# A masked-reconstruction loss on one core: the last columns taken singly, in parts and on another engine

## The chip, the cores and the metric

The kernel runs on one core of a Trainium2 chip. The time is that of the device for one execution, in microseconds. Nine runs of the kernel before have a median of 79.06 us (78.79 to 80.93). One further execution was recorded by the profiler; it took 79.05 us.

## The reference

Two float32 arrays `pred` and `target` of shape 32 x 147 x 768 come in, and 32 numbers go out, one for each batch entry:

```
mean = target.mean(axis=-1, keepdims=True)
var = target.var(axis=-1, keepdims=True)
target = (target - mean) / np.sqrt(var + 1e-6)
loss = np.mean((pred - target) ** 2, axis=-1)
return loss.mean(axis=-1).astype(np.float32)
```

Each of the 4,704 rows of 768 elements is normalised by its own mean and variance, the squared difference to `pred` is averaged over the row, and the 147 rows of an entry are averaged. Both inputs together are 28.9 MB, read once.

## The kernel before

**Tiling.** The 128 partitions hold 32 entries by 4 row groups. A "column" c is one row of 768 elements on each partition. There are 36 full columns, 0 to 35 (`KM` is 36), and one, `REST` = 36, of 96 partitions. So one column of one input is 393 KB in memory.

**Loads.** The list `stream` (lines 55 to 61) names the pieces in order: "t" for target, "p" for pred, first and last column, and the queue. The target's columns 36 and 0 to 3 come as float32 over SyncE's queue ("hw"). All others come over GpSimd's queue ("sw"), which casts them to bf16 on the way. Most pieces are four columns, the last of each input are two, and the pred columns 34 and 35 are single. There are eight completion semaphores for the sw loads, used in turn, which are called lanes here: a load waits on its lane until the load eight places before it has landed. It does so on GpSimd, where the next work queues behind it.

**The work on one column.** VectorE takes the statistics of the target (`stats`, lines 125 to 145: two `bn_stats` over 384 elements each, one `bn_aggr`). For a group of columns (`groups`: fours, and pairs from column 28 on) ScalarE takes the root of the variance and VectorE its reciprocal r, and the product nmr = -mean * r (line 144). GpSimd writes the normalised target to a bf16 tile s as target * r + nmr (`normalise`, line 158). TensorE forms pred minus s in PSUM with two products, by the negated identity `nident` for s and by the identity `ident` for pred (`subtract`, line 179). ScalarE squares the result in place and sums it along the row (`square`, line 185). A unit (`units`, line 63) is what one PSUM tile z and one square cover: two columns, except for 36, 34 and 35. There are two z tiles in turn. At the end TensorE adds the row sums by entry: products with a 0/1 mask that is scaled by 1/(147 * 768) (`sums`, lines 187 to 195). VectorE copies the 32 numbers out of PSUM (line 229) and SyncE stores them.

**Order.** Every instruction is put on record with a due time by `at`, from hand-set landing times and durations (lines 197 to 223), and all are issued in order of due time (line 225). Each engine runs its own queue strictly in that order, so an instruction that waits holds all behind it.

Of the kernel before, what the change touches and what calls it, by code (L numbers as in the profile page):

```python
# [14 lines left out]
def kernel(  # L15
# [24 lines left out]
    def rows_of(c):  # L40
        return RP if c == REST else P

    def dram(x, c0, c1):
        return bass.AP(tensor=x.tensor, offset=x.offset + c0 * D,
                       ap=[[N * D, B], [KJ * D, J - 1 if c0 == REST else J], [1, (c1 - c0) * D]])

    data = ctx.enter_context(tc.tile_pool(name="data", bufs=1))
    work = ctx.enter_context(tc.tile_pool(name="work", bufs=10))
    small = ctx.enter_context(tc.tile_pool(name="small", bufs=8))
# [2 lines left out]
    psum1 = ctx.enter_context(tc.tile_pool(name="psum1", bufs=1, space=bass.MemoryType.PSUM))  # L52


    stream = [("t", REST, REST + 1, "hw"), ("t", 0, 4, "hw"), ("p", REST, REST + 1, "sw")]
    stream += [("t", 4, 8, "sw"), ("t", 8, 12, "sw"), ("p", 0, 4, "sw")]
    for c in range(12, KM - 4, 4):
        stream += [("t", c, c + 4, "sw"), ("p", c - 8, c - 4, "sw")]
    stream += [("t", KM - 4, KM - 2, "sw"), ("p", KM - 12, KM - 8, "sw"), ("t", KM - 2, KM, "sw"),
               ("p", KM - 8, KM - 6, "sw"), ("p", KM - 6, KM - 4, "sw"), ("p", KM - 4, KM - 2, "sw"),  # L60
               ("p", KM - 2, KM - 1, "sw"), ("p", KM - 1, KM, "sw")]

    units = [(REST,)] + [(c, c + 1) for c in range(0, KM - 2, 2)] + [(KM - 2,), (KM - 1,)]

    groups = [(REST,)] + [tuple(range(c, c + 4)) for c in range(0, KM - 8, 4)]
    groups += [(c, c + 1) for c in range(KM - 8, KM, 2)]


    land, issue = {}, []
    t = 2.7  # L70
    for kind, c0, c1, q in stream:
        t += (c1 - c0) * D * 4 * rows_of(c0) / 430e3
        issue.append(t + 1.0)
        for c in range(c0, c1):
            land[kind, c] = t + 1.0

    todo = []

    def at(when, fn):
        todo.append((when, len(todo), fn))  # L80

    tbuf, pbuf, sbuf, rs = {}, {}, {}, {}

    def load(kind, c0, c1, q):
        x = targ_f if kind == "t" else pred_f
        n = rows_of(c0)
        til = data.tile([P, (c1 - c0) * D], F32 if q == "hw" else BF16, name=f"{kind}{c0}")
        eng = nc.sync if q == "hw" else nc.gpsimd
        pin(eng.dma_start(out=til[:n], in_=dram(x, c0, c1)))  # L89
        for c in range(c0, c1):  # L90
            (tbuf if kind == "t" else pbuf)[c] = (til, (c - c0) * D)

    lanes = [0.0] * 8
    k = 0
    for i, piece in enumerate(stream):
        if piece[3] == "hw":
            at(-1.0, lambda piece=piece: load(*piece))
        else:
            at(lanes[k % 8] + (0.01 * k), lambda piece=piece: load(*piece))
            lanes[k % 8] = issue[i] + 0.2  # L100
            k += 1

    ident = singles.tile([P, P], BF16)
    nident = singles.tile([P, P], BF16)
    mask = singles.tile([P, B], F32)
    mask_rest = singles.tile([P, B], F32)
    eps_t = singles.tile([P, 1], F32)

    def constants():
        pin(nc.vector.memset(eps_t, eps))  # L110
        for til, v in ((ident, 1.0), (nident, -1.0)):
            pin(nc.gpsimd.memset(til, 0.0))  # L112
            pin(nc.gpsimd.affine_select(out=til, in_=til, compare_op=ALU.not_equal, fill=v,  # L113
                                        base=0, pattern=[[-1, P]], channel_multiplier=1))
        for m, per, n in ((mask, J, P), (mask_rest, J - 1, RP)):
            pin(nc.gpsimd.memset(m, 1.0 / (N * D)))
            pin(nc.gpsimd.affine_select(out=m[:n], in_=m[:n], compare_op=ALU.is_ge, fill=0.0,
                                        base=0, pattern=[[-per, B]], channel_multiplier=1))
            pin(nc.gpsimd.affine_select(out=m[:n], in_=m[:n], compare_op=ALU.is_ge, fill=0.0,
                                        base=per - 1, pattern=[[per, B]], channel_multiplier=-1))  # L120

    at(1.0, constants)


    def stats(g):
        n, K = rows_of(g[0]), len(g)
        r = small.tile([P, K], F32, name="r")
        nmr = small.tile([P, K], F32, name="nmr")
        for i, c in enumerate(g):
            rs[c] = (r[:n, i:i + 1], nmr[:n, i:i + 1])  # L130
        if not norm_pix_loss:
            pin(nc.vector.memset(r, 1.0))
            pin(nc.vector.memset(nmr, 0.0))
            return
        mv = small.tile([P, K, 2], F32, name="mv")
        for i, c in enumerate(g):
            til, o = tbuf[c]
            st = small.tile([P, 2, 6], F32, name="st")
            for j in range(2):
                pin(nc.vector.bn_stats(out=st[:n, j, :], in_=til[:n, o + j * half:o + (j + 1) * half]))  # L140
            pin(nc.vector.bn_aggr(out=mv[:n, i], in_=st[:n]))  # L141
        pin(nc.scalar.activation(out=r[:n], in_=mv[:n, :, 1], func=ACTF.Sqrt, bias=eps_t[:n], scale=1.0))  # L142
        pin(nc.vector.reciprocal(out=r[:n], in_=r[:n]))  # L143
        pin(nc.vector.scalar_tensor_tensor(out=nmr[:n], in0=mv[:n, :, 0], scalar=-1.0,  # L144
                                           in1=r[:n], op0=ALU.mult, op1=ALU.mult))


    def normalise(u, i):
        c = u[i]
        n = rows_of(c)  # L150
        if i == 0:
            s = work.tile([P, 2 * D], BF16, name="s")
            for m, cc in enumerate(u):
                sbuf[cc] = (s, m * D)
        s, so = sbuf[c]
        til, o = tbuf[c]
        r, nmr = rs[c]
        pin(nc.gpsimd.tensor_scalar(out=s[:n, so:so + D], in0=til[:n, o:o + D], scalar1=r, scalar2=nmr,  # L158
                                    op0=ALU.mult, op1=ALU.add))


    main_units = [u for u in units if u[0] != REST]
    early = len(main_units) - 4
    rl = singles.tile([P, len(main_units)], F32)
    rl_rest = singles.tile([P, 1], F32)
    rl_sum = singles.tile([P, 1], F32)
    acc = psum1.tile([1, B], F32)
    zs = {}

    def subtract(u):  # L170
        n, W = rows_of(u[0]), len(u) * D
        z = psum.tile([P, 3 * BANK], F32, name="z")
        zs[u] = z
        s = sbuf[u[0]][0]
        ptil, po = pbuf[u[0]]
        for src, so, w, first in ((s, 0, nident, True), (ptil, po, ident, False)):
            for a in range(0, W, BANK):
                b = min(a + BANK, W)
                pin(nc.tensor.matmul(z[:n, a:b], w[:n, :n], src[:n, so + a:so + b], start=first, stop=not first))  # L179

    def square(u):
        n, W = rows_of(u[0]), len(u) * D
        z = zs[u]
        to = rl_rest[:n] if u[0] == REST else rl[:, main_units.index(u):main_units.index(u) + 1]
        pin(nc.scalar.activation(out=z[:n, :W], in_=z[:n, :W], func=ACTF.Square, accum_out=to))  # L185

    def sums(a, b):

        if a == "rest":
            pin(nc.tensor.matmul(acc, rl_rest[:RP], mask_rest[:RP], start=False, stop=False))  # L190
        elif a == 0:
            pin(nc.vector.tensor_reduce(out=rl_sum, in_=rl[:, 0:b], axis=mybir.AxisListType.X, op=ALU.add))  # L192
            pin(nc.tensor.matmul(acc, rl_sum, mask, start=True, stop=False))
        else:
            pin(nc.tensor.matmul(acc, rl[:, a:b], mask, start=False, stop=b == len(main_units)))  # L195

    dve = pool = pe = act = 0.0
    ready = {}
    for g in groups:
        dve = max([dve] + [land["t", c] for c in g])  # L200
        at(dve, lambda g=g: stats(g))
        dve += 1.26 * len(g) + 0.8
        for c in g:
            u = next(u for u in units if c in u)
            pool = max(pool, dve + 0.1)
            at(pool, lambda u=u, i=u.index(c): normalise(u, i))
            pool += 1.1
            ready[c] = pool + 0.1
    free = [0.0, 0.0]
    for u in units:  # L210
        pe = max([pe, free[0]] + [ready[c] for c in u] + [land["p", c] for c in u])
        at(pe, lambda u=u: subtract(u))
        pe += 0.7 * len(u)
        act = max(act, pe + 0.3)
        at(act, lambda u=u: square(u))
        act += 0.65 * len(u) + 0.35
        free = [free[1], act]
        i = main_units.index(u) if u in main_units else -1
        if i == early - 1:
            at(act + 3.0, lambda: sums(0, early))  # L220
            at(act + 3.0, lambda: sums("rest", None))
        elif i >= early:
            at(act + (3.1 if i < len(main_units) - 1 else 5.0), lambda i=i: sums(i, i + 1))

    for when, order, fn in sorted(todo, key=lambda e: e[:2]):
        fn()

    ob = singles.tile([1, B], F32)
    nc.vector.tensor_copy(out=ob, in_=acc)  # L229
    nc.sync.dma_start(out=out, in_=ob[0, :])  # L230


# [33 lines left out]
```

## Time and profile before

| | |
|---|---|
| median of nine runs | 79.06 us |
| the profiled execution | 79.05 us |
| its span, first to last instruction | 77.3 us |
| busy: TensorE, VectorE, ScalarE, GpSimd | 37.9, 45.9, 32.5, 50.3 us |
| read from memory | 28.90 MB |
| last input piece landed | 72.19 us |
| final product begins | 74.90 us |

The page's row "DMA" cuts the span into 40 slices of 1.93 us and shows the busy share of the 16 DMA engines in tenths. Lines of the timeline give start, duration, engine, source line, operation and tiles, and in brackets the idle time of the engine before it and what ended that. PE is TensorE, PEld its weight load, DVE is VectorE, ACT ScalarE, POOL GpSimd and SP SyncE. The landing of each load is read from the trace's semaphore records: a load has landed when the last of its 16 engines has reported.

### The profile page before, as it was taken

The numbers are of one execution on the slowest core, as the hardware profiler recorded it, in microseconds if no ns is written. First come the engines' busy times: TensorE is split into PE (matmuls) and PEld (weight loads), VectorE is DVE, ScalarE is ACT, GpSimd is POOL, SyncE is SP. The second block draws the span as 40 slices with busy tenths as digits, with TensorE's granted clock in tenths as the row PEclk, the third lists the DMA queues.
The fourth block names the chain that finished last, engine by engine and source line by source line (L and its number), as shares of the span: only waits on it lengthen the run. The fifth ranks groups of instructions, "written<-read, shape, count | busy, mean of one in ns | idle before, by whom it ended". The sixth has DMA issues, their size and how long they took to land.

```text
span 77.3 us, 601 instructions
## 1 busy us (share of the span) xinstructions
PE 37.9 (49%) x124; PEld 13.2 (17%) x126; DVE 45.9 (59%) x138; ACT 32.5 (42%) x53; POOL 50.3 (65%) x73
## 2 busy tenths in 40 slices
PE   0000250005990029979052982597079669467740
PEld 0000120001230013323011330232023123022310
DVE  0061009979979799799699339916797718400000
ACT  5001000050010194492790646095307395698960
POOL 4998902029959989899599699359887763180000
PEclk9999999999999655599975559857965999999999
DMA  0899999999999999999999999999999999997000
GB/s 0 184 407 299 312 238 219 210 216 213 219 210 223 207 216 217 216 213 213 216 213 219 210 216 217 216 216 210 203 223 223 197 210 213 218 199 128 2 0 0
DMA packets 3398, 15.43 MB, mean 200 GB/s; under 512 B 386, under 2 KB 738, under 8 KB 3266
## 3 DMA queue, kind: packets, MB, share of 16 engines
q0 software_dynamic: 3136, 13.52, 86.3%
q1 hardware_dynamic: 258, 1.87, 6.4%
q14 instruction: 3, 0.02, 0.1%
q8 instruction: 1, 0.02, 0.1%
HBM read 28.90 MB, written 0.00 MB: 374 GB/s over the span
## 4 chain that ended last, share of the span: by engine, by line
DMA 43%; DVE 32%; ACT 8%; POOL 5%; issue 5%; PE 2%; SPq 1%; another core or an unknown queue 0%; ACTq 0%
DMA p<-in_pred_dram 30%; DVE st L140 24%; DMA t<-in_target_dram 13%; ACT z L185 7%; DVE mv L141 5%; POOL s L158 4%; PE z L179 2%; ACT r L142 2%; DVE r L143 1%; DVE nmr L144 1%; SPq L89 1%; POOL t L89 1%; PE acc L195 0%; DVE ob L229 0%
## 5 line engine op out<-in xcount | busy, mean ns | idle before, releaser
L140 DVE BATCH_NORM_STATS2 st<-t 128x6 f32<-128x384 bf16 (+2 forms) x74 | 36.3, 533 | 14.4 <-DMA t<-in_target_dram 14.4
L158 POOL TENSOR_SCALAR s<-t,r,nmr 128x768 bf16<-128x768 bf16 (+2 forms) x37 | 36.1, 981 | 13.1 <-DVE nmr L144 12.8
L179 PE MATMUL z<-s,nident 128*128 128x512 bf16 (+3 forms) x57 | 21.2, 487 | 27.9 <-POOL s L158 25.0
L185 ACT ACTIVATE z<-z 128x1536 f32<-128x1536 f32 (+2 forms) x20 | 26.7, 1336 | 2.7 <-PE z L179 2.3
L179 PE MATMUL z<-p,ident 128*128 128x512 bf16 (+3 forms) x55 | 19.7, 472 | 8.5 <-DMA p<-in_pred_dram 8.3
L142 ACT ACTIVATE r<-mv,eps_t 128x4 f32<-128x4 f32 (+2 forms) x12 | 3.6, 297 | 38.9 <-DVE mv L141 38.9
L179 PEld LDWEIGHTS <-nident 128*128 128x128 bf16 (+1 forms) x57 | 5.9, 120 | 40.4 <-ACT z L185 16.3
L89 POOL DMA_DIRECT2D p<-in_pred_dram x13 | 7.7, 595 | 5.2 <-DMA t<-in_target_dram 3.2
L179 PEld LDWEIGHTS <-ident 128*128 128x128 bf16 (+1 forms) x57 | 6.8, 120 | 19.9 <-issue 17.1
L141 DVE BATCH_NORM_AGGREGATE mv<-st 128x2 f32<-128x12 f32 (+1 forms) x37 | 7.7, 209 | 1.3
L89 POOL DMA_DIRECT2D t<-in_target_dram x9 | 5.3, 590 | 0.0
L143 DVE RECIPROCAL r<-r 128x4 f32<-128x4 f32 (+2 forms) x12 | 2.1, 172 | 4.6 <-ACT r L142 4.6
L185 ACT ACTIVATION_READ_ACCUMULATOR z<-z 128x1 f32 (+1 forms) x20 | 3.7, 185 | 0.0
L229 DVE COPY ob<-acc 1x32 f32<-1x32 f32 x1 | 0.2, 178 | 5.3 <-PE acc L195 5.3
L144 DVE SCALAR_TENSOR_TENSOR nmr<-mv,r 128x4 f32<-128x4 f32 (+2 forms) x12 | 1.9, 161 | 0.4
L192 DVE TENSOR_REDUCE rl_sum<-rl 128x1 f32<-128x15 f32 x1 | 0.2, 169 | 2.6 <-ACT z L185 2.6
L142 ACT ACT_TABLE_LOAD x1 | 1.3, 1283 | 0.8 <-PEq L247 0.8
L195 PE MATMUL acc<-mask,rl 128*1 128x32 f32 x8 | 0.6, 192 | 0.8 <-ACT z L185 0.8
L110 DVE MEMSET eps_t<- 128x1 f32 x1 | 0.1, 59 | 0.9 <-PEq L247 0.9
L195 PEld LDWEIGHTS acc<-mask,rl 128*1 128x1 f32 x8 | 0.3, 82 | 1.2 <-ACT z L185 0.9
L112 POOL MEMSET ident<- 128x128 bf16 x1 | 0.4, 361 | 0.0
L113 POOL TENSOR_SCALAR_AFFINE_SELECT ident<-ident 128x128 bf16<-128x128 bf16 x1 | 0.3, 294 | 0.1
(16 smaller groups left out, 2.6 us busy)
## 6 DMA issues: line engine op xcount, KB each, us to landing
t<-in_target_dram POOLq DMA_DIRECT2D x7, 768.0 KB, 25.8
p<-in_pred_dram POOLq DMA_DIRECT2D x7, 768.0 KB, 26.4
t<-in_target_dram SPq DMA_DIRECT2D x1, 1536.0 KB, 9.9
p<-in_pred_dram POOLq DMA_DIRECT2D x3, 384.0 KB, 23.1
t<-in_target_dram POOLq DMA_DIRECT2D x2, 384.0 KB, 25.7
p<-in_pred_dram POOLq DMA_DIRECT2D x2, 192.0 KB, 16.5
t<-in_target_dram SPq DMA_DIRECT2D x1, 288.0 KB, 3.7
p<-in_pred_dram POOLq DMA_DIRECT2D x1, 144.0 KB, 3.7
```

The lines of the kernel that those rows point to most:

```text
L89: pin(eng.dma_start(out=til[:n], in_=dram(x, c0, c1)))
L112: pin(nc.gpsimd.memset(til, 0.0))
L113: pin(nc.gpsimd.affine_select(out=til, in_=til, compare_op=ALU.not_equal, fill=v, base=0, pattern=[[-1, P]], channel_multiplier=1))
L140: pin(nc.vector.bn_stats(out=st[:n, j, :], in_=til[:n, o + j * half:o + (j + 1) * half]))
L141: pin(nc.vector.bn_aggr(out=mv[:n, i], in_=st[:n]))
L142: pin(nc.scalar.activation(out=r[:n], in_=mv[:n, :, 1], func=ACTF.Sqrt, bias=eps_t[:n], scale=1.0))
L143: pin(nc.vector.reciprocal(out=r[:n], in_=r[:n]))
L144: pin(nc.vector.scalar_tensor_tensor(out=nmr[:n], in0=mv[:n, :, 0], scalar=-1.0, in1=r[:n], op0=ALU.mult, op1=ALU.mult))
L158: pin(nc.gpsimd.tensor_scalar(out=s[:n, so:so + D], in0=til[:n, o:o + D], scalar1=r, scalar2=nmr, op0=ALU.mult, op1=ALU.add))
L179: pin(nc.tensor.matmul(z[:n, a:b], w[:n, :n], src[:n, so + a:so + b], start=first, stop=not first))
L185: pin(nc.scalar.activation(out=z[:n, :W], in_=z[:n, :W], func=ACTF.Square, accum_out=to))
L195: pin(nc.tensor.matmul(acc, rl[:, a:b], mask, start=False, stop=b == len(main_units)))
```

## The change

- **Pieces of the stream.** The pred columns 20 to 27 are loaded by pairs, 30 to 34 singly. Column 35 is loaded as 512 and then 256 elements of each row, into tiles of their own. The target's columns 32 and 33 are moved ahead of the pred columns 20 to 23, and 34 and 35 to just behind these. Target 0 to 3 is put ahead of target 36.
- **Units.** Columns 30 to 35 are units of their own. Column 35 is two units of 512 and 256 elements, with a square each.
- **Columns 31 and 34 go to VectorE.** It writes pred minus s to a bf16 tile in SBUF, takes its mean and variance by `bn_stats` and `bn_aggr`, and forms mean squared plus variance. The mask for these two sums is `mask_mean`, which is `mask` times 768.
- **Scales.** The product nmr goes. ScalarE writes minus the mean (a Copy with scale -1) behind each root, and GpSimd computes (target - mean) * r. The groups of columns 28 to 35 are pairs, as before; their statistics, root and reciprocal are now separate steps that can be put between others.
- **Order.** The due times are replaced by a list planner: each step has an engine, a duration, the steps that it needs, a rank and an earliest time, and the step that can start first is issued next. The target product of a unit is a step of its own, and may run before the pred has landed.

In the planned order, VectorE's work at the end is the difference and statistics of column 31, the sum over the early units, and the difference and statistics of column 34. TensorE's ends with the two products of column 35's first part, the sums of columns 31 and 32, the two products of its second part, and the sums of 33, of both parts of 35 and of 34. ScalarE's order is: root of (34,35), squares of (26,27) and (28,29), and then of 30, 32, 33 and both parts of 35. GpSimd issues the loads of 30 to 35 one by one between the normalisations of columns 24 to 31.

```diff
-    stream = [("t", REST, REST + 1, "hw"), ("t", 0, 4, "hw"), ("p", REST, REST + 1, "sw")]
-    stream += [("t", 4, 8, "sw"), ("t", 8, 12, "sw"), ("p", 0, 4, "sw")]
+    piece("t", 0, 4, q="hw")
+    piece("t", REST, REST + 1, q="hw")
+    piece("t", 4, 8)
+    piece("p", REST, REST + 1)
+    piece("t", 8, 12)
+    piece("p", 0, 4)
     for c in range(12, KM - 4, 4):
-        stream += [("t", c, c + 4, "sw"), ("p", c - 8, c - 4, "sw")]
-    stream += [("t", KM - 4, KM - 2, "sw"), ("p", KM - 12, KM - 8, "sw"), ("t", KM - 2, KM, "sw"),
-               ("p", KM - 8, KM - 6, "sw"), ("p", KM - 6, KM - 4, "sw"), ("p", KM - 4, KM - 2, "sw"),
-               ("p", KM - 2, KM - 1, "sw"), ("p", KM - 1, KM, "sw")]
+        piece("t", c, c + 4)
+        if c == KM - 8:
+            piece("t", KM - 4, KM - 2)
+        if c < KM - 8:
+            piece("p", c - 8, c - 4)
+        else:
+            piece("p", c - 8, c - 6)
+            piece("p", c - 6, c - 4)
+    piece("t", KM - 2, KM)
+    for c in range(KM - 12, KM - 6, 2):
+        piece("p", c, c + 2)
+    for c in range(KM - 6, KM - 1):
+        piece("p", c, c + 1)
+    piece("p", KM - 1, KM, 0, BANK)
+    piece("p", KM - 1, KM, BANK, D)
...
-    units = [(REST,)] + [(c, c + 1) for c in range(0, KM - 2, 2)] + [(KM - 2,), (KM - 1,)]
+    units = [((c, c + 1), 0, D, "ACT") for c in range(0, KM - 6, 2)]
+    units.insert(2, ((REST,), 0, D, "ACT"))
+    units += [((KM - 6 + i,), 0, D, eng) for i, eng in enumerate(("ACT", "DVE", "ACT", "ACT", "DVE"))]
+    units += [((KM - 1,), 0, BANK, "ACT"), ((KM - 1,), BANK, D, "ACT")]
...
-        pin(nc.vector.scalar_tensor_tensor(out=nmr[:n], in0=mv[:n, :, 0], scalar=-1.0,
-                                           in1=r[:n], op0=ALU.mult, op1=ALU.mult))
+        pin(nc.scalar.activation(out=nm[:n], in_=mv[:n, :, 0], func=ACTF.Copy, scale=-1.0))
...
-        pin(nc.gpsimd.tensor_scalar(out=s[:n, so:so + D], in0=til[:n, o:o + D], scalar1=r, scalar2=nmr,
-                                    op0=ALU.mult, op1=ALU.add))
+        pin(nc.gpsimd.tensor_scalar(out=s[:n, so:so + D], in0=til[:n, o:o + D], scalar1=nm, scalar2=r,
+                                    op0=ALU.add, op1=ALU.mult))
...
+    def difference(u):
+        z = zs[u] = work.tile([P, D], BF16, name="zd")
+        s, so = sbuf[u[0]]
+        til, o = pred_of(u[0], 0)
+        pin(nc.vector.tensor_tensor(out=z, in0=til[:, o:o + D], in1=s[:, so:so + D], op=ALU.subtract))
+
+    def mean_of_squares(u, dest):
+        z = zs[u]
+        mv = small.tile([P, 2], F32, name="mvz")
+        bn(mv, [z[:, 0:half], z[:, half:D]])
+        pin(nc.vector.scalar_tensor_tensor(out=dest, in0=mv[:, 0:1], scalar=mv[:, 0:1], in1=mv[:, 1:2],
+                                           op0=ALU.mult, op1=ALU.add))
...
+    while left:
+        best = None
+        for i in left:
+            name, engine, dur, needs, fn, rank, early = ops[i]
+            if any(x not in end for x in needs):
+                continue
+            t = max([free[engine], early] + [end[x] + (0.0 if ops[by_name[x]][1] == engine else HOP) for x in needs])
+            key = (t, rank, i)
+            if best is None or key < best[0]:
+                best = (key, i)
```

## The prediction

> **What bounds the kernel now.** I read the page's span and DMA queues first, then the chain of waits, then the timeline of the last 15 us, then the busy times in short windows at the end.
>
> ```profile
> span 77.3 us, 601 instructions
> PE 37.9 (49%) x124; PEld 13.2 (17%) x126; DVE 45.9 (59%) x138; ACT 32.5 (42%) x53; POOL 50.3 (65%) x73
> DMA  0899999999999999999999999999999999997000
> ```
>
> No engine is above 65%, but the DMA row is at 9 from slice 2 to slice 35. Landing records of the trace: the 1.57 MB pieces of four columns land 3.66 us apart (30.95, 34.58, 38.24, 41.90), pairs 1.85 us (63.93 to 65.79), single columns 0.95 us, which fits 0.903 us a column plus 0.048 us a piece. The input stream is the bound. The last column, p35, lands at 72.19. What comes behind is the tail:
>
> ```profile
> 69.07 0.59 PE L179 MATMUL z<-p,ident 128*128 128x512 bf16 x2
> 69.98 1.44 ACT L185 ACTIVATE z<-z 128x1536 f32<-128x1536 f32 x1 [0.33 <-remote]
> 71.42 1.44 ACT L185 ACTIVATE z<-z 128x1536 f32<-128x1536 f32 x1
> 72.88 0.80 ACT L185 ACTIVATE z<-z 128x768 f32<-128x768 f32 x1
> 73.02 0.11 PEld L179 LDWEIGHTS <-nident 128*128 128x128 bf16 x2 [0.55 <-ACT z L185]
> 73.36 0.49 PE L179 MATMUL z<-p,ident 128*128 128x512 bf16 x2
> 73.95 0.80 ACT L185 ACTIVATE z<-z 128x768 f32<-128x768 f32 x1 [0.16 <-PE z L179]
> 74.66 0.20 ACT L185 ACTIVATION_READ_ACCUMULATOR z<-z 128x1 f32 x1
> 74.90 0.09 PEld L195 LDWEIGHTS acc<-mask,rl 128*1 128x1 f32 x2 [0.92 <-ACT z L185]
> 75.16 0.18 DVE L229 COPY ob<-acc 1x32 f32<-1x32 f32 x1 [5.31 <-PE acc L195]
> ```
>
> Each line is start, duration, engine, work; the bracket is idle time before it and its cause. ACT runs without a gap from 69.98: two pairs and two singles. p35 has lain there since 72.19, but its first matmul starts at 73.03, when the square of pair (32,33) frees the PSUM buffer. So the final matmul comes 2.71 us after the last landing (74.90 - 72.19), and the span ends 2.41 us after that. This is the part that the change can shorten. One more delay stands in front:
>
> ```profile
> 64.03 0.81 PE L179 MATMUL z<-p,ident 128*128 128x512 bf16 x3
> 66.44 0.30 ACT L142 ACTIVATE r<-mv,eps_t 128x2 f32<-128x2 f32 x1 [1.67 <-DVE mv L141]
> 66.64 1.43 ACT L185 ACTIVATE z<-z 128x1536 f32<-128x1536 f32 x1
> ```
>
> The square of (26,27) could start at 64.9, but in ACT's queue it stands behind the root for (34,35), whose target landed at 63.93. It starts at 66.64, so ACT enters the tail 1.7 us late.
>
> A second trait of the end: p30-31 lands at 69.03, though its first 15 engines are done by 67.7. At 67.00 the trace has a 16 KB instruction load of 945 ns on one DMA engine, and from there one engine is late: 1.39 us at p30-31, 0.76 at p32-33, p34 and p35. Without it p35 would have landed at 71.43.
>
> ```profile
> 70.00:71.00 1.00, 1.00 (x6) 0.32 (x4) 0.00 (x0) 1.00 (x1) 0.00 (x0) 1.00 0.83 153
> 71.00:71.50 0.50, 0.18 (x1) 0.00 (x0) 0.00 (x0) 0.50 (x3) 0.00 (x0) 1.00 0.08 12
> 71.50:72.00 0.50, 0.42 (x3) 0.30 (x4) 0.00 (x0) 0.50 (x2) 0.00 (x0) 1.00 0.05 9
> ```
>
> The last two numbers are DMA share and GB/s: from 71.0 on only about one engine of 16 still moves data.
>
> **The change, part by part.**
>
> *More pieces.* Loads go from 24 to 29: p20-23 and p24-27 split into pairs, p30-31 and p32-33 into singles, p35 into 512 and 256 elements a row. Five pieces at 0.048 us make 0.24 us on the stream, all on the path: p35's last part at 72.19 + 0.24 = 72.43. Working back by 0.903 us a column: first part of p35 72.08, p34 71.43, p33 70.48, p32 69.53. [...] At the lower end, no cost per piece, it is 0.24 us less.
>
> *Loads held by lanes.* A load waits for the landing of the one eight before it, on POOL, with the normalisations behind it queued. The new order makes this matter: p30 waits for t28-31 (52.9), p31 for t32-33, which is now ahead of p20 (54.7), p32 for p20-21 (56.6), p33 58.5, p34 for t34-35 (now 60.3), p35's parts for p24-25 (62.1) and p26-27 (64.0). POOL issues 0.3 us after a landing (12.60 to 12.89) and takes 0.58. So the last load is out at 64.0 + 0.9 = 64.9, seven columns before its turn (some 6 us of cover); a stall above that starves the stream one for one. Behind it stand four normalisations at 0.98: columns 32 to 35 done at 68.9. Column 35 is needed at 72.1 and 34 at 71.4, so there is over 2 us of slack.
>
> *Order of ACT.* t34-35 lands at 60.3 instead of 63.93, its stats end near 62.6 (two columns at 1.13), and its root stands behind the square of (24,25) at 64.5. The square of (26,27) follows near 65. The 1.7 us delay is gone, and ACT has caught up with the stream by (28,29): p28-29 lands at 65.9, square 66.8 to 68.3.
>
> *Scales.* The DVE product nmr (12 at 0.16 us) goes; ACT gets 12 small Copies, bounded by the root's 0.30 us, 3.6 us in all, hidden by ACT's 58% idle time; were it not hidden, one Copy (0.3) would stand before (26,27). DVE fills the root's latency (0.65 us a group before) with the next column's stats. The four-column target now goes first and t36 after it; t36's stats (1.13 us) move from idle time into DVE's early backlog, covered by six such gaps. DVE meets the loads near 38 us in both. Nothing of this reaches the end.
>
> *Two columns by DVE.* 31 and 34 leave PE and ACT (0.82 us of ACT each). On DVE each takes a 768-wide difference, two stats and an aggregate (1.02 + 0.24) and a small product (0.19). The difference has no row. By the nearest, stats at 533 ns for 384 elements, 768 would take at most 1.07. [...] Column 34: 71.47 + 0.56 + 0.05 + 1.02 + 0.24 + 0.19 = 73.53; with 1.07 it is 74.04, a quarter of a us behind the end worked out below. [...]
>
> *The last pieces.* First part of p35: matmul 72.12; from that to the square it was 0.59 with two matmuls (73.36 to 73.95), so 0.4 with one: square 72.5. Its length from the rows: 1536 takes 1.43 and 768 takes 0.80, so 0.82 ns an element and 0.17 fixed: 0.59 for 512, 0.38 for 256. On PE two sums (columns 31 and 32, some 0.25) and the second part's target product (0.25) stand between the two pred products: second pred product 72.9, square 73.25 to 73.63, accumulator out 73.75, final matmul 73.79. That is 1.11 us before 74.90, and column 34 on DVE (73.53) is ahead of it. The rest of the span is the same 2.41.
>
> Sum: 79.05 (the profiled run, span 77.3 and 1.75 around it; the median is 79.06) - 1.11 = **77.9**.
>
> **The rivals.**
>
> *A. The stream's late engine isn't there,* because the instruction load falls elsewhere. Then all pieces land 0.76 us earlier, ACT isn't late, and the final matmul comes near 73.03: gain 1.87, 77.2. For it: instructions per engine change. Against: PE's list is nearly as long (231 rows for 233) and reaches the same place. If the load hits the last two microseconds it costs up to 1.39 instead of 0.76: 78.2 to 78.5.
>
> [...]
>
> *C. Slower: the stream is starved.* POOL holds loads by lanes between normalisations, and a late piece of the target stalls both. Every us the 16 engines stand idle is a us at the end; it outweighs the gain from 1.1 us of idle time and shows from 1.5 us. For it: POOL has five more issues and now waits for lanes at the end. Against: 6 us of cover at the last load and over 10 before that. At 2.5 us idle: 80.4.
>
> **How the numbers follow.** As summed, 0.52 (77.5 to 78.3); A 0.24 (77.0 to 77.4, or to 78.5 with a later instruction load); B 0.11; C 0.13. What a measurement here can tell from no change is about 0.5%, 78.66 to 79.46. Faster: 0.52 + 0.24 + a third of B = 0.80; same: the rest of B = 0.07; slower: C = 0.13. The range runs from A's no-cost end, 76.9, to the top of B, 79.2, and leaves C out.
>
> **What would show it.** Right: last landing at 71.7 to 72.5; final matmul 1.2 to 1.5 us behind it (before 2.71); no ACT gap before the square of (26,27) of more than the Copy; the difference near 0.56 us; DMA row at 9 to the same slice. Wrong: DMA slices below 9 before the end (C), the last sum waiting for DVE or ACT for over half a us (B), POOL's last normalisation after 71.

## The result

The changed kernel takes 77.82 us (median of 10 runs, 77.60 to 78.34), the kernel before 79.04 (31 runs). The ratio is 0.9846 with a 95% interval of 0.9823 to 0.9868: 1.5% faster, some 1.2 us, where 77.9 was forecast. The profiled execution has a span of 75.9 us instead of 77.3; with 77.60 us it is the fastest of the ten, while the profiled execution of the kernel before (79.05) stands at the median, so the traces show about 0.2 us more gain than the medians. In experiment 8 the profiled execution was a disturbed one of 110 us, so that only its ratio enters the comparisons.

The page of the changed kernel, the same three rows as before:

```profile
span 75.9 us, 637 instructions
PE 38.7 (51%) x127; PEld 12.0 (16%) x128; DVE 50.0 (66%) x137; ACT 32.2 (42%) x67; POOL 52.6 (69%) x78
DMA  0899999999999999999999999999999999999600
```

The stream is full to about the same time as before. The landing records say it finer: the last input piece is in at 72.18, against 72.19 before. So the transfers gained nothing, and all of the gain lies behind them. The end of the timeline of the changed kernel:

```profile
69.86 0.49 PE L226 MATMUL z<-p,ident 128*128 128x512 bf16 x2 [0.76 <-DMA p<-in_pred_dram]
70.44 0.80 ACT L238 ACTIVATE z<-z 128x768 f32<-128x768 f32 x1 [1.08 <-PE z L226]
71.24 0.80 ACT L238 ACTIVATE z<-z 128x768 f32<-128x768 f32 x1
71.28 0.56 DVE L245 TENSOR_TENSOR zd<-p,s 128x768 bf16<-128x768 bf16 x1 [0.24 <-DMA p<-in_pred_dram]
72.21 0.22 PE L294 MATMUL acc<-mask_mean,rl 128*1 128x32 f32 x2
72.37 0.58 ACT L238 ACTIVATE z<-z 128x512 f32<-128x512 f32 x1 [0.22 <-PE z L226]
72.53 0.27 PE L226 MATMUL z<-p,ident 128*128 128x256 bf16 x1
72.96 0.38 ACT L238 ACTIVATE z<-z 128x256 f32<-128x256 f32 x1
73.17 0.22 DVE L251 SCALAR_TENSOR_TENSOR rl<-mvz 128x1 f32<-128x1 f32 x1
73.44 0.22 PE L294 MATMUL acc<-mask_mean,rl 128*1 128x32 f32 x2
73.50 0.22 PE L294 MATMUL acc<-mask,rl 128*1 128x32 f32 x2
73.76 0.18 DVE L322 COPY ob<-acc 1x32 f32<-1x32 f32 x1 [0.37 <-PE acc L294]
```

Before, ScalarE had no gap of more than 0.16 us from 69.98 on, and the final product came 2.71 us after the last landing. Now ScalarE waits for the stream (1.08 us idle before the square of column 32), and the final product at 73.50 comes 1.32 us after the landing. VectorE's sum of column 34 (73.39) and ScalarE's last square (73.34, with its accumulator read out at 73.45) end level. That is 1.40 us less at the final product, and 2.39 us follow it to the end of the span, as before (2.41).

### The profile page after: what moved, and what is told of

It reads as the page before. It is cut to its first block, busy times and chain, and to the rows that moved or that the text cites. A ratio compares the mean times of both kernels' runs of the same rounds, so it can differ in the third digit from the quotient of the medians.

```text
span 75.9 us, 637 instructions
## 1 busy us (share of the span) xinstructions
PE 38.7 (51%) x127; PEld 12.0 (16%) x128; DVE 50.0 (66%) x137; ACT 32.2 (42%) x67; POOL 52.6 (69%) x78
## 4 chain that ended last, share of the span: by engine, by line
DMA 62%; DVE 13%; POOL 13%; issue 3%; PE 2%; ACT 2%; POOLq 0%; DVEq 0%; ACTq 0%
DMA p<-in_pred_dram 51%; DMA t<-in_target_dram 11%; POOL s L212 10%; DVE st L162 10%; POOL p L108 2%; PE z L226 2%; ACT z L238 2%; DVE mv L163 2%; DVE zd L245 1%; POOL t L108 1%; PE acc L294 0%; DVE r L192 0%; DVE rl L251 0%; DVE mvz L163 0%; ACT r L186 0%
## 5 line engine op out<-in xcount | busy, mean ns | idle before, releaser
L212 POOL TENSOR_SCALAR s<-t,nm,r 128x768 bf16<-128x768 bf16 (+2 forms) x37 | 36.0, 979 | 10.0 <-DVE r L192 7.8
L238 ACT ACTIVATE z<-z 128x1536 f32<-128x1536 f32 (+4 forms) x21 | 25.7, 1223 | 22.5 <-PE z L226 22.5
L226 PE MATMUL z<-s,nident 128*128 128x512 bf16 (+3 forms) x55 | 19.9, 472 | 24.3 <-POOL s L212 17.5
L226 PEld LDWEIGHTS <-nident 128*128 128x128 bf16 (+1 forms) x55 | 4.8, 110 | 38.5 <-ACT z L238 16.8
L108 POOL DMA_DIRECT2D p<-in_pred_dram x18 | 10.3, 575 | 0.7 <-issue 0.4
L245 DVE TENSOR_TENSOR zd<-p,s 128x768 bf16<-128x768 bf16 x2 | 1.9, 956 | 2.9 <-POOL s L212 2.6
L151 DVE TENSOR_SCALAR mask_mean<-mask 128x32 f32<-128x32 f32 x1 | 2.6, 2644 | 0.0
L187 ACT ACTIVATE nm<-mv 128x4 f32<-128x4 f32 (+2 forms) x12 | 2.3, 190 | 0.0
L162 DVE BATCH_NORM_STATS2 st<-zd 128x6 f32<-128x384 bf16 x4 | 2.0, 552 | 0.1
L294 PE MATMUL acc<-mask,rl 128*1 128x32 f32 x10 | 1.1, 191 | 0.2 <-ACT z L238 0.2
```

The source lines that it names most:

```text
L108: pin((nc.sync if q == "hw" else nc.gpsimd).dma_start(out=til[:n], in_=src))
L151: op("mask_mean", "DVE", 0.2, ["masks"], lambda: pin(nc.vector.tensor_scalar(out=mask_mean, in0=mask, scalar1=float(D), scalar2=None, op0= ...
L162: pin(nc.vector.bn_stats(out=st[:n, j, :], in_=x))
L187: pin(nc.scalar.activation(out=nm[:n], in_=mv[:n, :, 0], func=ACTF.Copy, scale=-1.0))
L226: pin(nc.tensor.matmul(z[:n, a:b], eye[:n, :n], src[:n, so + a:so + b], start=first, stop=not first))
L238: pin(nc.scalar.activation(out=z[:n, :w], in_=z[:n, :w], func=ACTF.Square, accum_out=dest[:n]))
```

## The experiments

Times are medians; where a time is compared with the changed kernel it is by the ratios to the kernel before, times 79.04.

**1. Columns 31 and 34 back on ScalarE.**

```diff
-("ACT", "DVE", "ACT", "ACT", "DVE")
+("ACT", "ACT", "ACT", "ACT", "ACT")
```

> The changed kernel with columns 31 and 34 back on TensorE and ScalarE. Theory (the gain is the shortened tail, and VectorE's share is one of its parts): two more squares of 0.82 us stand in ScalarE's queue; worked through by queues, the square of column 34 ends near 73.1 instead of not being there, the two parts of column 35 follow it at 73.1 and 73.95, and the final product comes near 74.5 instead of 73.5. The time is 1.0 us above the changed kernel, 78.8 us. Rival (ScalarE has slack, the stream alone sets the end): at most 0.2 us, 78.0.

78.44 us, ratio 0.9928 (0.9915 to 0.9941): 0.65 us of the gain is lost. The end of its timeline:

```profile
71.42 0.80 ACT L238 ACTIVATE z<-z 128x768 f32<-128x768 f32 x1
72.39 0.80 ACT L238 ACTIVATE z<-z 128x768 f32<-128x768 f32 x1
73.19 0.59 ACT L238 ACTIVATE z<-z 128x512 f32<-128x512 f32 x1
73.81 0.37 ACT L238 ACTIVATE z<-z 128x256 f32<-128x256 f32 x1
74.34 0.22 PE L294 MATMUL acc<-mask,rl 128*1 128x32 f32 x2 [0.18 <-ACT z L238]
```

The queue is the one that was worked out (column 34's square ends at 73.19, 73.1 said), but the last square starts 0.14 us earlier than said, and the final product comes 0.84 us behind the changed kernel's by the two profiles, 0.65 by the medians, where 1.0 was said; the two differ because the changed kernel's profiled execution lay 0.22 us under its median. ScalarE has no slack at the end, and VectorE's share is the largest single part of the gain.

**2. Column 35 whole.**

```diff
-    piece("p", KM - 1, KM, 0, BANK)
-    piece("p", KM - 1, KM, BANK, D)
+    piece("p", KM - 1, KM)
...
-    units += [((KM - 1,), 0, BANK, "ACT"), ((KM - 1,), BANK, D, "ACT")]
+    units += [((KM - 1,), 0, D, "ACT")]
```

> The changed kernel with column 35 loaded in one piece and squared in one unit. Theory: the one piece lands 0.05 us earlier, but its square of 0.80 us starts only 0.6 us behind the landing and nothing of it is done before: final product near 73.8, so +0.3 us, 78.1. Rival (the split of the last column is the main source of the gain): +0.8 us or more. Rival (the split costs more on the stream than it saves): 0 or faster.

78.12 us, ratio 0.9899 (0.9865 to 0.9933): 0.4 us above the changed kernel, 0.3 expected; the two intervals touch (0.9865 and 0.9868). The piece lands at 72.28, and all of the work on column 35's pred comes after it:

```profile
72.33 0.48 PE L225 MATMUL z<-p,ident 128*128 128x512 bf16 x2 [0.22 <-DMA p<-in_pred_dram]
72.91 0.80 ACT L237 ACTIVATE z<-z 128x768 f32<-128x768 f32 x1 [0.69 <-PE z L225]
73.86 0.22 PE L293 MATMUL acc<-mask,rl 128*1 128x32 f32 x2
```

**3. Columns 30 to 33 in pairs.**

```diff
-    for c in range(KM - 12, KM - 6, 2):
+    for c in range(KM - 12, KM - 2, 2):
         piece("p", c, c + 2)
-    for c in range(KM - 6, KM - 1):
-        piece("p", c, c + 1)
+    piece("p", KM - 2, KM - 1)
...
-    units += [((KM - 6 + i,), 0, D, eng) for i, eng in enumerate(("ACT", "DVE", "ACT", "ACT", "DVE"))]
+    units += [((KM - 2,), 0, D, "DVE")]
```

> The changed kernel with columns 30 to 33 loaded and squared in pairs on ScalarE, column 34 on VectorE alone, column 35 in two parts as in the changed kernel. Theory: two pieces fewer give 0.1 us back on the stream, but the square of (32,33) takes 1.43 us from about 71.25 and both parts of column 35 queue behind it: final product near 73.9, +0.4 us, 78.2. Rival (column 34 and the split of 35 are all that counts): 0, 77.8.

78.12 us, ratio 0.9881 (0.9861 to 0.9900): 0.3 us above the changed kernel, with intervals that overlap a little. The edit also gives column 31 back to ScalarE, so it is not the pieces alone. The trace shows the mechanism: the pair (32,33) is in at 70.32, its square is long, and the first part of column 35 stands behind it.

```profile
71.26 1.44 ACT L237 ACTIVATE z<-z 128x1536 f32<-128x1536 f32 x1 [1.06 <-PE z L225]
72.70 0.59 ACT L237 ACTIVATE z<-z 128x512 f32<-128x512 f32 x1
73.54 0.37 ACT L237 ACTIVATE z<-z 128x256 f32<-128x256 f32 x1
```

The last square starts 0.25 us after the one before has ended. In this execution TensorE's clock was at half from 72.5 us on, and the second part's product was done only at 73.44; about that much of this execution's loss is not the pair's.

**4. The kernel before, with the last root behind the square of (26,27).** The root, reciprocal and product of columns 34 and 35 are issued as a step of their own.

```diff
+        if g == (KM - 2, KM - 1):
+            held.append(lambda: scales(n, r, nmr, mv))
+        else:
+            scales(n, r, nmr, mv)
...
         at(act, lambda u=u: square(u))
+        if u == (KM - 10, KM - 9):
+            at(act, lambda: held[0]())
```

> The kernel before, with only the last root on ScalarE (columns 34 and 35) moved behind the square of (26,27), so that this square starts near 64.9 instead of 66.64. Theory: nothing, 79.0 within 0.1 us, since the square of (30,31) waits for its pred, which lands at 69.03, whether ScalarE came late or not. Rival (the late root is a main part of what the change gains): 0.5 us or more faster, 78.5.

78.68 us, ratio 0.9970 (0.9949 to 0.9991): 0.24 us faster. Both readings miss, and my reason fell with its number: p30-31 did not land at 69.03 here but at 67.73. The 16 KB instruction load came at 67.14 instead of 67.00, and the first pair with one engine late is p32-33 (69.93): by these times the load fell behind p30-31 on its DMA engine. So ScalarE stood in front of (32,33), not of (30,31), and its early start counted for something:

```profile
65.02 1.44 ACT L193 ACTIVATE z<-z 128x1536 f32<-128x1536 f32 x1 [0.16 <-PE z L187]
68.67 1.44 ACT L193 ACTIVATE z<-z 128x1536 f32<-128x1536 f32 x1
70.88 1.44 ACT L193 ACTIVATE z<-z 128x1536 f32<-128x1536 f32 x1 [0.66 <-PE z L187]
```

How much of the 0.24 us is the root and how much the last landing (71.86 here, 72.19 before) one profile doesn't tell.

**5. The first four pieces in the order of before.**

```diff
-    piece("t", 0, 4, q="hw")
     piece("t", REST, REST + 1, q="hw")
-    piece("t", 4, 8)
+    piece("t", 0, 4, q="hw")
     piece("p", REST, REST + 1)
+    piece("t", 4, 8)
```

> The changed kernel with the first four pieces in the order of before (target 36 ahead of target 0 to 3, pred 36 ahead of target 4 to 7). In the profile of the changed kernel target 4 to 7 landed at 12.78 instead of 12.60. Theory (the stream is the bound from its first piece, so what it loses at the start is still missing at the end): 0.17 us faster than the changed kernel, 77.65. Rival (the early order is covered, since VectorE and not the stream is behind then): 0, 77.8; or slower, if target 36's statistics in its idle time no longer pay.

77.88 us, ratio 0.9859 (0.9822 to 0.9897), no different from the changed kernel. Fifteen engines did finish 0.33 us earlier (71.52 for 71.85), but the sixteenth was the last at 72.32 (72.18 before the edit). And TensorE's clock was at half from 70.7 us on, so that column 35's first product took 0.59 us instead of 0.38. The rival's number came in; its reason, cover by VectorE, isn't what the trace shows.

**6. Pred 20 to 27 in fours, planner untouched.**

```diff
-        if c < KM - 8:
-            piece("p", c - 8, c - 4)
-        else:
-            piece("p", c - 8, c - 6)
-            piece("p", c - 6, c - 4)
+        piece("p", c - 8, c - 4)
...
-    for c in range(KM - 12, KM - 6, 2):
-        piece("p", c, c + 2)
+    piece("p", KM - 12, KM - 8)
+    piece("p", KM - 8, KM - 6)
```

> The changed kernel with pred columns 20 to 27 in two pieces of four columns, as before, and not in four of two. The planner, left as it is, then puts the sum of column 34 (VectorE) ahead of the last two products on TensorE. Theory: two pieces less give 0.1 us back, but the products of the second part of column 35 now wait for VectorE's sum of column 34 near 73.3, and its square comes after: final product near 74.2, +0.6 us, 78.4. [...] Rival (TensorE's order at the end is covered): -0.1 us, 77.7.

79.00 us, ratio 0.9996 (0.9977 to 1.0015): the whole gain is gone, twice what was expected. In the traced execution two things end level. One is the wait that I named: VectorE has the sum of column 34 at 73.53, its product on TensorE begins at 73.59, and behind it stand the products of column 35's second part, the last of which begins at 74.00. The other is ScalarE, which takes the last square at 74.36, the moment it is through with the one before. It had been without a gap of over a quarter of a us since 66.31:

```profile
PEclk9999999999999999975555555555555555589999
...
64.72 2.77 PE L222 MATMUL z<-p,ident 128*128 128x512 bf16 x6
66.31 1.44 ACT L234 ACTIVATE z<-z 128x1536 f32<-128x1536 f32 x1 [2.60 <-PE z L222]
...
73.31 0.22 DVE L247 SCALAR_TENSOR_TENSOR rl<-mvz 128x1 f32<-128x1 f32 x1
73.59 0.22 PE L290 MATMUL acc<-mask_mean,rl 128*1 128x32 f32 x2
74.00 0.27 PE L222 MATMUL z<-p,ident 128*128 128x256 bf16 x1
74.36 0.37 ACT L234 ACTIVATE z<-z 128x256 f32<-128x256 f32 x1
74.89 0.22 PE L290 MATMUL acc<-mask,rl 128*1 128x32 f32 x2 [0.18 <-ACT z L234]
```

The first row is from its page: the granted clock of TensorE, in tenths, over the 40 slices. It was at half from about 34 to 68 us. The six products for columns 24 to 27 took 2.77 us, and ScalarE began their squares 1.5 us later than in run 7.

A ScalarE on time would not have helped much. In the changed kernel the last pred product begins 0.32 us after a sum that stands ahead of it (72.21 to 72.53); here its square follows 0.36 us later and the final product 0.53 us after that. From 73.59 on this makes an estimated 74.80 for the final product, where 74.89 was measured and the changed kernel has 73.50. And the loss does not need the slow clock of the traced execution: all twelve executions took 78.6 to 79.2 us, with a mean granted clock from 0.78 (the traced one) to 0.90; the ten of the changed kernel took 77.6 to 78.3 us at 0.81 to 0.91.

**7. The same with the sums held.** The sums of columns 31 to 35 need the last product of column 35 to have been issued.

```diff
-    op(("final", i), "PE", 0.2, [need, "masks", "mask_mean"], ...
+    op(("final", i), "PE", 0.2, [need, "masks", "mask_mean"] + ([("pred", len(units) - 1)] if i > 2 else []), ...
```

> The run with pred 20 to 27 in fours once more, but with the sums of columns 31 to 35 held on TensorE until the last product has been issued. In the run without this, ScalarE had no gap from 66.31 to the end, and the clock of TensorE was at half from 54 to 68 us. Theory now (the four columns 24 to 27 land together at 64.07, so ScalarE gets two squares at once and is behind from there; the sum of column 34 on TensorE only took a place in a queue that ScalarE held anyway): 78.9, no different from that run within 0.2 us. Rival (the sum of column 34 ahead of the last products was the cause): 77.7 to 77.9.

77.84 us, ratio 0.9847 (0.9816 to 0.9878): the rival, and the changed kernel's time. My theory, that four columns landing together are the cause, is refuted. (The half-speed stretch of run 6 that it names begins at 34 us, not at 54.) The clock row and the six products of this run:

```profile
PEclk9999999999999999997589559857999559999999
...
63.91 1.46 PE L222 MATMUL z<-p,ident 128*128 128x512 bf16 x6 [0.41 <-DMA p<-in_pred_dram]
64.82 1.44 ACT L234 ACTIVATE z<-z 128x1536 f32<-128x1536 f32 x1 [1.65 <-PE z L222]
```

The same six products take 1.46 us at full clock. In the two traces every engine but TensorE has the same instructions in the same order, and TensorE too if its sums are left out. So the 1.2 us hang on where the sums stand. By the estimate above and the clocks of the twelve executions, the likely cause is the wait of the last products behind VectorE's sum of column 34. The traces alone don't part it from the clock: the traced execution of run 6 had both, that of run 7 neither, and no execution of run 6 at a faster clock was traced.

**8. First pieces as before, fours, sums held.** Edits 5, 6 and 7 together.

> The changed kernel with the first pieces as before, pred 20 to 27 in fours, and the sums of columns 31 to 35 held on TensorE until the last product has been issued. Theory: 0.17 + 0.10 us less on the stream and no new wait: 77.55, 0.27 us faster than the changed kernel. Rival: the five small products that are now behind the last one hold the end by 0.1 to 0.3 us, 77.7 to 77.9.

Ratio 0.9854 (0.9814 to 0.9893): 77.9 us by the ratio, no better than the changed kernel. The theory's 77.55 is not reached.

**9. VectorE takes 32 and 34.**

```diff
-("ACT", "DVE", "ACT", "ACT", "DVE")
+("ACT", "ACT", "DVE", "ACT", "DVE")
```

> The changed kernel with VectorE taking column 32 instead of 31, and 34 as in the changed kernel. Theory (VectorE's column 34 is level with ScalarE's last square, so VectorE has no slack): column 32 is in at 69.8 at the earliest, its 2.1 us end near 71.9, column 34 follows with 2.1 us, near 74.0, and with the sum of the early columns behind it the final product comes near 74.3: +0.7 us, 78.5. The difference takes 0.56 us both times, since GpSimd is done by then, against 1.35 for column 31 in the changed kernel. Rival (the 1.35 us of column 31's difference beside GpSimd holds the end): faster than the changed kernel.

78.46 us, ratio 0.9907 (0.9868 to 0.9945): about 0.5 us above the changed kernel, 0.7 expected. VectorE becomes the end, as worked out:

```profile
69.92 0.56 DVE L245 TENSOR_TENSOR zd<-p,s 128x768 bf16<-128x768 bf16 x1 [4.70 <-DMA p<-in_pred_dram]
71.95 0.55 DVE L245 TENSOR_TENSOR zd<-p,s 128x768 bf16<-128x768 bf16 x1
73.34 0.19 ACT L238 ACTIVATION_READ_ACCUMULATOR z<-z 128x1 f32 x1
74.11 0.22 PE L294 MATMUL acc<-mask_mean,rl 128*1 128x32 f32 x2 [0.70 <-DVE rl L251]
```

ScalarE is done at 73.5, and the last sums wait 0.7 us for VectorE. The differences take 0.56 and 0.55 us with GpSimd idle (its last normalisation ends at 68.93); the long difference of column 31 (below) was covered in the changed kernel.

**10. Scales as before, in the changed kernel.** No Copy; VectorE forms nmr.

```diff
-        pin(nc.scalar.activation(out=nm[:n], in_=mv[:n, :, 0], func=ACTF.Copy, scale=-1.0))
...
             pin(nc.vector.reciprocal(out=rs[g][:n], in_=rs[g][:n]))
+            pin(nc.vector.scalar_tensor_tensor(out=rs[g, 1][:n], in0=mvs[g][:n, :, 0], scalar=-1.0,
+                                               in1=rs[g][:n], op0=ALU.mult, op1=ALU.mult))
...
```

> The changed kernel with the scales as before: no Copy on ScalarE, the product nmr on VectorE behind the reciprocal, GpSimd with r and nmr. Theory (covered work): 0 within 0.2 us, 77.8. Rival (the Copy on ScalarE takes from the gain, or VectorE needed the relief): more than 0.3 us either way.

78.00 us, ratio 0.9875 (0.9844 to 0.9907): 0.2 us above, with intervals that overlap. Covered, as far as this can be told; a cost of 0.2 us isn't excluded.

**11. The kernel before with the middle of the stream changed.**

```diff
-    for c in range(12, KM - 4, 4):
-        stream += [("t", c, c + 4, "sw"), ("p", c - 8, c - 4, "sw")]
-    stream += [("t", KM - 4, KM - 2, "sw"), ("p", KM - 12, KM - 8, "sw"), ("t", KM - 2, KM, "sw"),
-               ("p", KM - 8, KM - 6, "sw"),
+    for c in range(12, KM - 8, 4):
+        stream += [("t", c, c + 4, "sw"), ("p", c - 8, c - 4, "sw")]
+    stream += [("t", KM - 8, KM - 4, "sw"), ("t", KM - 4, KM - 2, "sw"), ("p", KM - 16, KM - 14, "sw"),
+               ("p", KM - 14, KM - 12, "sw"), ("t", KM - 2, KM, "sw"), ("p", KM - 12, KM - 10, "sw"),
+               ("p", KM - 10, KM - 8, "sw"), ("p", KM - 8, KM - 6, "sw"),
...
```

> The kernel before, with only the middle of the stream as in the change: target 32 to 35 ahead, and pred 20 to 27 in pairs; the last six columns, the planner and the scales are those of before. Theory (this part brings ScalarE to the tail in time, as moving the root did, and the rest of the gain is the finer tail): root of (34,35) near 62.9, square of (32,33) from 70.9, of 34 from 72.4 and of 35 from 73.4, final product 74.35 instead of 74.90: 0.5 us faster than before, 78.5. Rival (all of the gain is the finer tail): 0 to 0.1 us slower, 79.1. Rival (all of the gain is the stream's order): 77.9.

79.12 us, ratio 1.0012 (0.9995 to 1.0030): nothing. The run didn't do what it was meant to. The order of before puts the last root ahead of five squares, and its statistics end at 64.5, where I had put the root itself near 62.9, so that ScalarE is held as before:

```profile
64.64 0.30 ACT L143 ACTIVATE r<-mv,eps_t 128x2 f32<-128x2 f32 x1 [1.33 <-DVE mv L142]
64.84 1.43 ACT L186 ACTIVATE z<-z 128x1536 f32<-128x1536 f32 x1
```

It shows that an earlier target alone gains nothing; it doesn't tell what it is worth with ScalarE's order put right.

**12. First pieces as before and sums held.** Edits 5 and 7.

> The changed kernel with the first pieces in the order of before and the sums of columns 31 to 35 held until the last product has been issued. Theory: 0.17 us less on the stream, and the second part's products no longer behind two sums of 0.25 us: 77.6. Rival (the stream's start is recovered or lost again by the instruction load and by TensorE's clock, whose half-speed stretches moved by several us from run to run): 77.8 to 78.0, no better than the changed kernel.

77.81 us, ratio 0.9842 (0.9811 to 0.9872): the rival, no better than the changed kernel. No run beat it by more than its interval.

## Why the prediction was right

*The bound and the tail.* Shown. The last landing didn't move and the tail went from 2.71 to 1.32 us; undoing VectorE's share, the split of 35 and the single columns 30 to 33 one at a time gives back 0.65, 0.4 and 0.3 us, together about the whole gain. The parts overlap (the third run also takes column 31 from VectorE), and two of the three differences are near the size of their intervals. That 77.9 met the median so closely is in part luck: the sum was worked out for the profiled execution, and that one took 77.60.

*More pieces.* The term that was mis-sized. I put 0.24 us on the path and kept the late engine's 0.76, so 72.43 for the last landing; it was 72.18. The price of a piece was about right: on the mean of the 16 engines the last piece lands 0.28 us later (71.44 for 71.16), of which 0.06 is there already at target 4 to 7 (12.27 for 12.21), and 0.22 is left for five more pieces. But the late engine was only 0.33 us behind the fifteenth to finish (72.18 and 71.85), and before 0.78 (72.19 and 71.41). Over all profiles but that of experiment 8, with 24 to 29 pieces, the last engine finishes between 71.86 and 72.40 and the fifteenth between 71.41 and 72.35. So the price of the pieces showed on the other engines and hardly on the one that ends the stream; why that one was less late is open. The second part of column 35, 131 KB, landed 0.32 us behind the first in the full queue (72.18 and 71.86), where the sum had 0.35.

*Loads held by lanes.* The last load was out at 65.09 (64.9 said), the normalisations done at 69.00 (68.9). The DMA row stays at 9 until the last pieces, so rival C had no part.

*Order of ACT.* Square of (26,27) at 65.23 (near 65), of (28,29) at 67.00 (66.8). That the delay was worth removing is less sure than I had it: in the kernel before, moving the root alone gained 0.24 us, and part of that may be an earlier landing.

*Two columns by DVE.* The difference of column 34 took 0.56 us, as the sum has it, and not the 1.07 of the row of statistics; its sum ended at 73.39 (73.53). No row of the kernel before shows the 0.56, it was an estimate of mine; in the traces of the runs every difference that starts after GpSimd's last normalisation takes 0.55 or 0.56 us. Beside the normalisations the difference of column 31 took 1.35 us:

```profile
65.13 3.87 POOL L212 TENSOR_SCALAR s<-t,nm,r 128x768 bf16<-128x768 bf16 x4
...
68.06 1.35 DVE L245 TENSOR_TENSOR zd<-p,s 128x768 bf16<-128x768 bf16 x1 [2.62 <-POOL s L212]
```

In the changed kernel column 31's difference starts at 68.06 and ends 0.41 us after GpSimd's last normalisation (69.00): 0.79 us longer than column 34's, less than one normalisation (0.98), and covered. Where it starts just after the last normalisation has ended (67.93 in run 6, 67.73 in run 7), it takes 0.56 us.

*The last pieces.* Squares at 72.37 and 72.96 (72.5 and 73.25 said), final product 73.50 (73.79). Most of the 0.29 us is the landing (0.25).

*The scales* were covered, as far as run 10 can tell. I left out one instruction: `mask_mean`, which took 2.64 us (below). VectorE was in its early backlog then and waited for a load again at 38.4 us, so it cost nothing at the end.

*Rivals.* A came true in part: the instruction load did not go away, it came at 67.78 instead of 67.00, and what it cost at the last landing went from 0.76 to 0.33. (TensorE's list, which I had as 231 rows for 233, has 255 rows for 250 in the traces.) B is a tail that isn't shortened, by what small pieces cost or by a VectorE sum ahead of the last product. No run shows the cost that its 79.2 rests on for the pieces; five more took 0.22 us (above). For the sum, the changed kernel has only that of column 31 there, which is done at 70.96. With the sum of column 34 there too (run 6) the time was 79.0, near that 79.2, and with the sums held back (run 7) it was 77.84. So the wait for the sum is likely a real one, which the order of the changed kernel avoids.

## What to carry to other kernels

When the input stream is the bound, look at what is left to do after the last byte: cut the last pieces finer, and give some of the last columns to an engine that is idle then, until the engines end level. A piece more costs 0.05 us here (0.22 us for five), less than the work that it lets start early. Look at the order of the last small instructions too: with one sum of VectorE ahead of TensorE's last products the whole 1.2 us were gone (79.00 us in run 6, 77.84 with the sums held in run 7). Read the granted clock beside such a comparison, and the clocks of all executions, not of the traced one alone: the trace of run 6 had a slow clock, but its other executions lost as much without so slow a one.

## What the runs showed of the hardware that was not expected

- Some VectorE operations took far longer beside GpSimd's normalisations than without them, also a very small one. `mask_mean`, 128 x 32 elements, in the changed kernel:

```profile
28.34 2.91 POOL L212 TENSOR_SCALAR s<-t,nm,r 128x768 bf16<-128x768 bf16 x3
...
28.64 2.64 DVE L151 TENSOR_SCALAR mask_mean<-mask 128x32 f32<-128x32 f32 x1
```

It starts beside three normalisations in a row and ends at 31.28, with the last of them (31.25). In runs 5 and 12 the same instruction begins in a gap between two normalisations (at 29.52 and 29.91) and takes 0.13 us. In run 10 the product nmr, 0.16 us in the kernel before, took 1.47 and 1.76 us in the two cases where it ran beside normalisations near the end.

- TensorE's granted clock goes between full and half in every profile but that of experiment 8. The half-speed stretches last 3.41 us or a multiple of it (those that run past the end of the span aside), and where they fall differs: from 34 to 68 us in run 6, from 70.7 us to the end of the work in run 5, not at all after 63 us in the changed kernel. It differs from one execution to the next as well: the mean clock of the changed kernel's ten executions goes from 0.81 to 0.91. What sets the stretches off, no run here shows.

- A 16 KB instruction load, 0.89 to 0.95 us on one DMA engine, falls between 67.0 and 68.3 us in all profiles but that of experiment 8 (there it comes at 83.5). From there on one engine's share of each piece lands late: by 1.4 us at pred 30-31 in the kernel before, and at the last piece by 0.04 to 0.8 us against the fifteenth engine (in run 12, where it is 0.04, two engines are late). That the load makes it late is read from the times alone: the records don't name the engine, nor do they say which engine's instructions the load brings, and no run took it away.
